# Few-key attention weights of two query blocks through one transpose, and the indexer's last pair in another PSUM pool

## The chip, the cores and the metric

The kernel runs on one core of one Trainium2 chip. The metric is the device time of one execution in microseconds (us), lower is better. A core has five instruction queues that run side by side, each strictly in its own order: TensorE (PE, matmuls, with its weight loads listed as PEld), VectorE (DVE), ScalarE (ACT), GpSimd (POOL) and SyncE (SP, which issues most transfers). Matmul results land in PSUM, which this kernel divides into eight buffers of 128 x 512 fp32: four "big" ones (pool `pm`, tile `mm`) and four "small" ones (pool `pa`, tile `at`).

## What is computed

One decoder layer on 256 tokens and 16 learned meta tokens in front of them (272 rows, width 2048). Cut to what the change touches:

```python
q, c_kv, q_idx, k_idx, w_idx, u = split_columns(h @ w_in)
score = einsum('bqhs,bqh->bqs', relu(q_idx . k_idx), w_idx)     # 16 indexer heads
_, sel = top_k(where(causal, score, -1e30), 64)
logits = q_abs . c_sel * HEAD_DIM**-0.5 + rel_bias[bucket(dist)]
p = softmax(logits);  o = p . c_sel;  attn = o @ w_uv           # 8 heads of 128
h = LN(alpha*h + concat(attn, pooled) @ w_o)                    # then a gated MLP and a second LN
```

The MLP (5632 wide, twice up and once down) is the larger part of the work; the change lies in the attention in front of it.

## The kernel before, in words

**Numbers.** Every fp32 product of the weights is made of three fast matmuls: operand a is split into a rounded upper part and the rest, and upper x upper, upper x rest and rest x upper are added in PSUM. Weights come from memory in blocks of 128 x 2048 (`wraw`); ACT writes the upper part (L127, two halves per block), DVE the rest (L128, two halves) into a ring of three `whl` buffers. `product` (L193) then issues 16 x 3 matmuls per block (L199, L200, L201). This runs through the whole kernel.

**Order.** The Tile layer places the instructions: it decides which buffer of a pool each tile gets, and in which order each queue holds its instructions. It is not written out by hand, so an edit of one tile can move others.

**Start.** PE runs 13 matmuls on a zeroed tile `warm` (L85 to L89) until the first input has been loaded and split. The first input blocks carry indexer key, head weights and the key/value latent (L264).

**Indexer.** Eight products, each for a pair of indexer heads, with the dots of the pair before in between (`dots`, L352: per head one matmul pair for each of the two query blocks, two ReLU copies on ACT, two accumulations on DVE into `score`). The eighth pair's dots come in the middle of the key projection (L403), in small buffers, like the projection itself (`kt`, L401).

**Two query blocks.** Queries 0 to 127 (block A) see 16 meta keys and 128 token keys (KA = 144); queries 128 to 255 (block B) see all 272 (KB). `score`, `bias` and the logits hold A's 144 columns and then B's 272 in one 416-wide row. The 64 largest scores per query are struck out in eight rounds on DVE (L444 to L448), L450 finds which are gone, and L452 adds -1e30 to the bias of the others, one instruction per head. The bias itself was laid out, mirrored, by three transfers (L345).

**Values.** `v0`, `v1`, `v2` (L413 to L439) are the values of the 16 meta keys, of the next 128 and of the last 128. `v0` holds the 16 rows three times, from partitions 0, 32 and 64 on (upper, rest, upper), in a zeroed tile of 80 rows; its counterpart for the weights, `ptx`, holds upper, upper, rest. One matmul with 80 rows gives all three products.

**Head loop (L585 to L611).** Eight heads, one per pass. In each pass PE runs one product for the pooling half of the layer (48 matmuls) and, between its slices, the attention steps of neighbouring heads: the logits of the next head (`softmax`, L489), `values` of the last head (L523) and `turn` of this head (L504). `softmax` scales and biases on DVE (L494), finds the largest logit per block (L497, A before B), ACT takes the exponential with its sum (L498), DVE divides (L501). `turn` transposes on PE: three 128 x 128 pieces (L506 to L508), and the 16 meta-key columns of A (L509) and of B (L510). ACT copies the big pieces (`pts`, L512) and the small ones twice into `ptx` (L518), DVE forms the rest (L520), POOL zeroes `ptx` first (L515). `values` (L526 to L528) multiplies them with `v0`, `v1`, `v2`. The pooling half follows in the same pass: ACT copies the finished product out (`u`, L549), POOL adds up windows (L553), DVE subtracts (L559), ACT and DVE split (L563, L564), and `pooled` (L566) multiplies every second pass. ACT then splits the next weight block (L127).

## Time and profile before

| | |
|---|---|
| median of 3 runs | 1045.23 us (1044.82 to 1045.94) |
| the profiled execution | 1045.81 us |
| its span, first to last instruction | 1044.0 us |
| mean granted TensorE clock | 0.997 |
| DVE, ACT, POOL busy | 85%, 60%, 19% of the span |

The profile is of one execution, so sums are made against its own 1045.81 us, 1.8 us of which lie outside the span; it is 0.6 us above the median. A matmul's row shows its whole latency; matmuls overlap, so what one costs is the distance from its start to the next start. In rows of a timeline the columns are start, length (of all that are merged), engine, line, operation, operands, shapes and count, then the idle time in front and what ended it. The head loop lies between about 140 and 211 us of the span, the indexer before 83 us, the MLP after about 304 us.

### The profile page before, as it was taken

The numbers are of one execution on the slowest core, as the hardware profiler recorded it, in microseconds if no ns is written. First come the engines' busy times: TensorE is split into PE (matmuls) and PEld (weight loads), VectorE is DVE, ScalarE is ACT, GpSimd is POOL, SyncE is SP. The second block draws the span as 40 slices with busy tenths as digits, with TensorE's granted clock in tenths as the row PEclk, the third lists the DMA queues.
The fourth block names the chain that finished last, engine by engine and source line by source line (L and its number), as shares of the span: only waits on it lengthen the run. The fifth ranks groups of instructions, "written<-read, shape, count | busy, mean of one in ns | idle before, by whom it ended". The sixth has DMA issues, their size and how long they took to land.

```text
span 1044.0 us, 19202 instructions
## 1 busy us (share of the span) xinstructions
PE 1034.6 (99%) x7639; PEld 984.2 (94%) x7639; DVE 888.2 (85%) x1401; ACT 623.2 (60%) x1000; POOL 194.8 (19%) x248
## 2 busy tenths in 40 slices
PE   9999999999999999999999999999999999999997
PEld 8999999999999999989999999999999999999986
DVE  6879568758779997799989989899898999999876
ACT  6666446645448855456565655656555666555665
POOL 1200014125340021211112111120111201220031
PEclk9999999999999999999999999999999999999998
DMA  8755643454554578789887787877878878787865
GB/s 319 256 180 216 226 145 117 146 189 164 180 196 149 175 223 238 235 291 298 278 285 274 262 291 267 287 273 269 281 268 287 275 277 278 268 286 270 292 214 159
DMA packets 59754, 250.28 MB, mean 240 GB/s; under 512 B 21734, under 2 KB 22416, under 8 KB 32656
## 3 DMA queue, kind: packets, MB, share of 16 engines
q1 hardware_dynamic: 34592, 230.42, 61.1%
q0 software_dynamic: 7888, 16.14, 8.2%
q10 hardware_dynamic: 17184, 2.49, 1.5%
q8 instruction: 60, 0.98, 0.4%
q14 instruction: 30, 0.25, 0.1%
HBM read 232.50 MB, written 2.11 MB: 225 GB/s over the span
## 4 chain that ended last, share of the span: by engine, by line
PE 85%; DVE 6%; issue 3%; DMA 3%; ACT 2%; POOL 1%; SPq 0%; POOLq 0%; DVEq 0%; ACTq 0%
PE mm L200 21%; PE mm L199 21%; PE mm L201 21%; PE at L785 5%; PE at L784 5%; PE at L786 5%; DVE whl L128 3%; DMA wraw<-in_w_first 1%; DMA wraw<-in_w_down 1%; ACT whl L127 1%; DMA wraw<-in_w_up 1%; DVE hp L705 0%; DVE x L700 0%; DVE x L701 0%; PE at L358 0%
## 5 line engine op out<-in xcount | busy, mean ns | idle before, releaser
L128 DVE TENSOR_TENSOR whl<-wraw,whl 128x1024 fp32r<-128x1024 f32 (+1 forms) x416 | 488.5, 1208 | 39.5 <-ACT whl L127 38.7
L127 ACT ACTIVATE whl<-wraw 128x1024 fp32r<-128x1024 f32 (+1 forms) x416 | 402.9, 1015 | 115.5 <-issue 27.1
L200 PE MATMUL mm<-hp,whl 128*128 128x258 f32 x1280 | 362.4, 283 | 0.7 <-DVE hp L705 0.7
L199 PE MATMUL mm<-hp,whl 128*128 128x258 f32 x1280 | 361.4, 282 | 0.0
L201 PE MATMUL mm<-hp,whl 128*128 128x258 f32 x1280 | 361.2, 282 | 0.0
L200 PEld LDWEIGHTS mm<-hp,whl 128*128 128x128 f32 x1280 | 242.7, 190 | 4.0 <-DVE hp L705 0.9
L199 PEld LDWEIGHTS mm<-hp,whl 128*128 128x128 f32 x1280 | 242.5, 189 | 3.2
L201 PEld LDWEIGHTS mm<-hp,whl 128*128 128x128 f32 x1280 | 242.9, 190 | 0.1
L199 PE MATMUL mm<-xp,whl 128*128 128x256 f32 (+5 forms) x384 | 111.9, 291 | 0.0
L200 PE MATMUL mm<-xp,whl 128*128 128x256 f32 (+5 forms) x384 | 108.7, 283 | 0.0
L201 PE MATMUL mm<-xp,whl 128*128 128x256 f32 (+5 forms) x384 | 108.7, 283 | 0.0
L719 ACT ACTIVATE z<-mm,cv 128x256 f32<-128x256 f32 x40 | 22.5, 563 | 95.6 <-PE mm L201 95.6
L199 PEld LDWEIGHTS mm<-xp,whl 128*128 128x128 f32 x384 | 72.4, 189 | 1.0 <-issue 0.5
L200 PEld LDWEIGHTS mm<-xp,whl 128*128 128x128 f32 x384 | 72.3, 188 | 0.4
L201 PEld LDWEIGHTS mm<-xp,whl 128*128 128x128 f32 x384 | 72.4, 188 | 0.3 <-DVE whl L128 0.2
L785 PE MATMUL at<-whl,gp 128*128 128x512 f32 x180 | 71.2, 396 | 0.8 <-DVE whl L128 0.8
L786 PE MATMUL at<-whl,gp 128*128 128x512 f32 x180 | 71.0, 395 | 0.0
L784 PE MATMUL at<-whl,gp 128*128 128x512 f32 x180 | 69.4, 395 | 0.0
L719 ACT ACTIVATE za<-mm,cv 128x256 f32<-128x256 f32 x40 | 22.5, 562 | 70.9 <-PE mm L201 66.2
L759 POOL TENSOR_TENSOR forms<-za 128x128 f32<-128x128 f32 x20 | 23.3, 1167 | 203.5 <-DVE za L737 203.5
L756 POOL TENSOR_TENSOR forms<-za 128x128 f32<-128x128 f32 x20 | 21.2, 1059 | 203.5 <-DVE za L737 139.1
L786 PEld LDWEIGHTS at<-whl,gp 128*128 128x128 f32 x180 | 33.8, 188 | 7.8
(346 smaller groups left out, 1925.4 us busy)
## 6 DMA issues: line engine op xcount, KB each, us to landing
wraw<-in_w_up SPq DMA_DIRECT2D x88, 1024.0 KB, 5.0
wraw<-in_w_down SPq DMA_DIRECT2D x80, 1024.0 KB, 6.8
wraw<-in_w_proj SPq DMA_DIRECT2D x24, 1024.0 KB, 5.0
wraw<-in_w_o SPq DMA_DIRECT2D x16, 1024.0 KB, 4.9
y<-v POOLq DMA_DIRECT2D x27, 256.0 KB, 8.5
y<-u POOLq DMA_DIRECT2D x18, 256.0 KB, 4.7
wraw<-in_w_first SPq DMA_DIRECT2D x8, 304.0 KB, 5.5
x<-in_xt SPq DMA_DIRECT2D x1, 2176.0 KB, 8.9
```

Source lines behind the costliest of these rows:

```text
L127: upper = nc.scalar.activation(hl[:, 0, c], raw[:, c], AF.Copy)
L128: lower = nc.vector.tensor_tensor(hl[:, 1, c], raw[:, c], hl[:, 0, c].bitcast(F32), op=ALU.subtract)
L199: nc.tensor.matmul(ps, wh, ah, start=n == 0, stop=False)
L200: nc.tensor.matmul(ps, wh, al, start=False, stop=False)
L201: nc.tensor.matmul(ps, wl, ah, start=False, stop=n == KT - 1)
L719: nc.scalar.activation(z, src[:, 2:NQ], AF.Identity, bias=col(C_B, j), scale=col(C_W, 3 * j + 2))
L756: nc.gpsimd.tensor_tensor(s[:, 0], a21, a22, op=ALU.add)
L759: nc.gpsimd.tensor_tensor(s[:, 3], a11, a21, op=ALU.subtract)
L784: nc.tensor.matmul(ps, a[:, 0, i], hl[:, 0, w], start=j == 0, stop=False)
L785: nc.tensor.matmul(ps, a[:, 0, i], hl[:, 1, w], start=False, stop=False)
L786: nc.tensor.matmul(ps, a[:, 1, i], hl[:, 0, w], start=False, stop=j == n - 1)
```

## The change

The diff does five things. Line numbers of the profile are those of the kernel before.

- **Warm-up:** the matmuls at the start read a constant that the program makes anyway, and there are 14 of them.
- **Last indexer pair:** its dots go to `big` buffers, not `small` ones.
- **Layout:** the 416-wide rows are B then A, so that B's 16 meta keys stand at the end of its 272 columns, right before A's 16 meta keys. For that `kt` gets the meta keys a second time at its end (a POOL copy), the bias has four transfers, and L450 becomes three instructions that put the pieces in the new order (`out_of`).
- **Turn:** one transpose of 32 columns replaces L509 and L510. Its 32 result rows are B's meta keys and A's; both blocks' columns need only one half of them. So `ptx` and `v0` have 96 rows, all written, in place of 80 with zeroed gaps; each copy is made per query block with a scale per partition (`of_block`, ones or zeros) that blanks the other block's rows: four ACT copies of 32 x 128 for two of 16 x 256, and two DVE instructions of 32 x 128 for one of 16 x 256. POOL's zeroing of `ptx` goes.
- **First two queries:** their weights (`lm`) get a row of 32 with zeros in its first half.

The order of PE's instructions is as before outside three places: the dots of the last pair, three matmuls of the first query product that now stand among the value matmuls, and the turn. On DVE the top-k rounds are no longer interrupted by two halves of a weight block (L128); one of them now stands right before the eight bias instructions and the other right behind. On ACT the exponential of the 272-wide block comes before that of the 144-wide one, and all four copies of a turn stand where the two stood.

```diff
@@ -82,10 +82,9 @@
         return pa.tile([P, 512], F32, tag="at", name="at")
 
 
-    warm = sb.tile([P, 256], mybir.dt.bfloat16, name="warm")
-    nc.gpsimd.memset(warm, 0.0)
+    warm = nc.const_aps.tensor(1.0, (P, 256), mybir.dt.bfloat16)
     ps = small()
-    for _ in range(13):
+    for _ in range(14):
         nc.tensor.matmul(ps[:, :256], warm[:, :P], warm, start=True, stop=True)
 
 
@@ -288,8 +287,9 @@
                                 compare_op=ALU.is_ge, fill=NEG, base=t0, channel_multiplier=1)
 
 
-    kt = ap_.tile([P, H, T], F32, name="kt")
-    ct = kt[:, H - 2:, :]
+
+    kt = ap_.tile([P, H, T + NM], F32, name="kt")
+    ct = kt[:, H - 2:, :T]
     sqs = []
     for j in range(2):
         ps = heads[1 + j][0]
@@ -342,18 +342,19 @@
         nc.vector.tensor_copy(strip[:, P:], ps[:H, :T])
         strip_d = dram.tile([H, STRIP], F32, name="strip_d")
         nc.gpsimd.dma_start(strip_d, strip)
-        for dst, n_rows, t0, n in ((bias[:, :, :KB], P, NM + P, KB), (bias[:, :, KB:], P, NM, KA), (bias_m, 2, Q0, NM)):
-
-            src = bass.AP(tensor=strip_d.tensor, offset=strip_d.offset + P + t0 - (n - 1),
+        for dst, n_rows, t0, s0, n in ((bias[:, :, :KA], P, NM, 0, KA), (bias[:, :, KA:KA + NM], P, NM + P, 0, NM),
+                                       (bias[:, :, KA + NM:], P, NM + P, NM, KB - NM), (bias_m, 2, Q0, 0, NM)):
+
+            src = bass.AP(tensor=strip_d.tensor, offset=strip_d.offset + P + t0 - s0 - (n - 1),
                           ap=[[1, n_rows], [STRIP, H], [1, n]])
             nc.gpsimd.dma_start(dst, src)
 
 
-    def dots(j, qi, pa_, heads):
+    def dots(j, qi, pa_, heads, buffer=small):
 
         for i in heads:
             h = 2 * j + i
-            pb = small()
+            pb = buffer()
             for o, n, t in ((pa_[:, S * i:S * i + S], S, slice(0, P)), (pb[:, :T], T, slice(P, S))):
                 nc.tensor.matmul(o, qi[:, i, t], kidx[:, 0, :n], start=True, stop=False)
                 nc.tensor.matmul(o, qi[:, i, t], kidx[:, 1 + i, :n], start=False, stop=True)
@@ -398,44 +399,46 @@
             nc.tensor.matmul(ps[:, :T], uk[:, 0, w], ctp[:, c, 0, :], start=c == 0, stop=False)
             nc.tensor.matmul(ps[:, :T], uk[:, 0, w], ctp[:, c, 1, :], start=False, stop=False)
             nc.tensor.matmul(ps[:, :T], uk[:, 1, w], ctp[:, c, 0, :], start=False, stop=c == 1)
-        nc.scalar.activation(kt[:, h, :], ps[:, :T], AF.Copy)
+        nc.scalar.activation(kt[:, h, :T], ps[:, :T], AF.Copy)
         if h == 2:
-            dots(7, qis[7], small(), (0, 1))
+            dots(7, qis[7], big(), (0, 1), big)
+    nc.gpsimd.tensor_copy(kt[:, :, T:], kt[:, :, :NM])
 
     y = sb.tile([P, KT, T], F32, tag="y", name="x", padded_shape=[P, KT, T])
     nc.sync.dma_start(y, xt)
     uv = weights()
 
-    few = ap_.tile([P, 2, 48], F32R, name="few")
-    nc.gpsimd.memset(few.bitcast(F32), 0.0)
-    for p in range(2):
-        nc.gpsimd.tensor_copy(few[:, :, 32 * p:32 * p + NM], ctp[:, :, p, :NM])
+    few = ap_.tile([P, 2, 4, NM], F32R, name="few")
+    for p in range(4):
+        nc.gpsimd.tensor_copy(few[:, :, p, :], ctp[:, :, p // 2, :NM])
     vs = []
     for i, (a, b) in enumerate(((0, NM), (NM, NM + P), (NM + P, T))):
         if i:
             v = ap_.tile([b - a, 1024], F32, name=f"v{i}", tag=f"v{i}")
         else:
 
-            v = ap_.tile([80, 1024], F32R, name="v0")
-            nc.gpsimd.memset(v.bitcast(F32), 0.0)
+            v = ap_.tile([96, 1024], F32R, name="v0")
         for g in range(2):
             ps = small()
             for c in range(2):
                 w = slice(1024 * c + 512 * g, 1024 * c + 512 * g + 512)
                 if i == 0:
-                    nc.tensor.matmul(ps[:48], few[:, c, :], uv[:, 0, w], start=c == 0, stop=False)
-                    nc.tensor.matmul(ps[:48], few[:, c, :], uv[:, 1, w], start=False, stop=c == 1)
+                    stack = few[:, c].rearrange("p a b -> p (a b)")
+                    nc.tensor.matmul(ps[:64], stack, uv[:, 0, w], start=c == 0, stop=False)
+                    nc.tensor.matmul(ps[:64], stack, uv[:, 1, w], start=False, stop=c == 1)
                     continue
                 nc.tensor.matmul(ps[:b - a], ctp[:, c, 0, a:b], uv[:, 0, w], start=c == 0, stop=False)
                 nc.tensor.matmul(ps[:b - a], ctp[:, c, 0, a:b], uv[:, 1, w], start=False, stop=False)
                 nc.tensor.matmul(ps[:b - a], ctp[:, c, 1, a:b], uv[:, 0, w], start=False, stop=c == 1)
             w = slice(512 * g, 512 * g + 512)
-            nc.scalar.activation(v[:b - a, w], ps[:b - a], AF.Copy)
-            if i == 0:
-                low = v[32:32 + NM, w]
-                nc.vector.tensor_tensor(low, ps[:NM], v[:NM, w].bitcast(F32), op=ALU.subtract)
-                nc.vector.tensor_tensor(low, ps[32:32 + NM], low.bitcast(F32), op=ALU.add)
-                nc.scalar.activation(v[64:64 + NM, w], ps[:NM], AF.Copy)
+            if i:
+                nc.scalar.activation(v[:, w], ps[:b - a], AF.Copy)
+            else:
+                low = v[32:64, w]
+                for r in (0, 64):
+                    nc.scalar.activation(v[r:r + 32, w], ps[:32], AF.Copy)
+                nc.vector.tensor_tensor(low, ps[:32], v[:32, w].bitcast(F32), op=ALU.subtract)
+                nc.vector.tensor_tensor(low, ps[32:64], low.bitcast(F32), op=ALU.add)
         vs.append(v)
 
 
@@ -447,9 +450,11 @@
             nc.vector.max(m8, src[:, a:b])
             nc.vector.match_replace(out=work[:, a:b], in_to_replace=m8, in_values=src[:, a:b], imm_value=REPLACED)
         src = work
-    nc.vector.tensor_tensor(work, work, score, op=ALU.is_equal)
+    out_of = temp([P, KW], "out_of")
+    for to, a, b in ((0, KA + NM, KW), (KB - NM, KA, KA + NM), (KB, 0, KA)):
+        nc.vector.tensor_tensor(out_of[:, to:to + b - a], work[:, a:b], score[:, a:b], op=ALU.is_equal)
     for h in range(H):
-        nc.vector.scalar_tensor_tensor(bias_of(h), work, NEG, bias_of(h), op0=ALU.mult, op1=ALU.add)
+        nc.vector.scalar_tensor_tensor(bias_of(h), out_of, NEG, bias_of(h), op0=ALU.mult, op1=ALU.add)
 
 
     qt = ap_.tile([P, H, NQ], F32, name="qt", tag="q")
@@ -464,7 +469,9 @@
     ps = small()
     for h in range(H):
         nc.tensor.matmul(ps[:2, h * NM:(h + 1) * NM], qt[:, h, :2], kt[:, h, :NM], start=True, stop=True)
-    lm = ap_.tile([2, H, NM], F32, name="lm")
+    both_few = temp([2, H * 2 * NM], "lm").rearrange("p (a b) -> p a b", b=2 * NM)
+    nc.gpsimd.memset(both_few, 0.0)
+    lm = both_few[:, :, NM:]
     nc.vector.scalar_tensor_tensor(lm, ps[:2, :H * NM].rearrange("p (a b) -> p a b", b=NM), scale,
                                    bias_m[:, :, ::-1], op0=ALU.mult, op1=ALU.add)
     mm = ap_.tile([2, 2, H], F32, name="mmeta")
@@ -474,50 +481,56 @@
     nc.vector.tensor_reduce(mm[:, 1, :], lm, axis=AX.X, op=ALU.add)
     nc.vector.reciprocal(mm[:, 1, :], mm[:, 1, :])
     nc.vector.tensor_tensor(lm, lm, mm[:, 1, :, None].to_broadcast([2, H, NM]), op=ALU.mult)
-    pm_sb = ap_.tile([NM, H, 2], F32, name="pm_sb")
+
+    pm_sb = ap_.tile([2 * NM, H, 2], F32, name="pm_sb")
+    of_block = ap_.tile([2 * NM, 2], F32, name="of_block")
+    for i in range(2):
+        nc.vector.tensor_reduce(of_block[:, i:i + 1], ident[:2 * NM, NM * i:NM * i + NM], axis=AX.X, op=ALU.add)
 
     def meta_weights():
         pmeta = small()
         for h in range(H):
-            nc.tensor.transpose(pmeta[:NM, 2 * h:2 * h + 2], lm[:, h, :], ident[:2, :2])
-        nc.vector.tensor_copy(pm_sb.rearrange("p a b -> p (a b)"), pmeta[:NM, :2 * H])
+            nc.tensor.transpose(pmeta[:2 * NM, 2 * h:2 * h + 2], both_few[:, h, :], ident[:2, :2])
+        nc.vector.tensor_copy(pm_sb.rearrange("p a b -> p (a b)"), pmeta[:2 * NM, :2 * H])
 
 
     mix = [None] * KT
-    AB = ((0, KA), (KA, KW))
+    BA = ((0, KB), (KB, KW))
 
     def softmax(h):
         ps = big()
-        nc.tensor.matmul(ps[:, :KA], qt[:, h, 2:2 + P], kt[:, h, :KA], start=True, stop=True)
-        nc.tensor.matmul(ps[:, KA:KW], qt[:, h, 2 + P:], kt[:, h, :], start=True, stop=True)
+        nc.tensor.matmul(ps[:, KB:KW], qt[:, h, 2:2 + P], kt[:, h, :KA], start=True, stop=True)
+        nc.tensor.matmul(ps[:, :KB], qt[:, h, 2 + P:], kt[:, h, NM:], start=True, stop=True)
         lg = temp([P, KW], "lg")
         nc.vector.scalar_tensor_tensor(lg, ps[:, :KW], scale, bias_of(h), op0=ALU.mult, op1=ALU.add)
         st = ap_.tile([P, 3, 2], F32, name="st", tag="st", bufs=2)
-        for i, (a, b) in enumerate(AB):
+        for i, (a, b) in enumerate(BA):
             nc.vector.tensor_reduce(st[:, 0, i:i + 1], lg[:, a:b], axis=AX.X, op=ALU.max, negate=True)
             nc.scalar.activation(lg[:, a:b], lg[:, a:b], AF.Exp, bias=st[:, 0, i:i + 1], accum_out=st[:, 1, i:i + 1])
         nc.vector.reciprocal(st[:, 2, :], st[:, 1, :])
-        for i, (a, b) in enumerate(AB):
+        for i, (a, b) in enumerate(BA):
             nc.vector.tensor_scalar_mul(lg[:, a:b], lg[:, a:b], st[:, 2, i:i + 1])
         return lg
 
     def turn(h, lg):
         pt, ptm = small(), small()
-        nc.tensor.transpose(pt[:, :P], lg[:, NM:KA], ident)
-        nc.tensor.transpose(pt[:, P:2 * P], lg[:, KA + NM:KA + NM + P], ident)
-        nc.tensor.transpose(pt[:, 2 * P:3 * P], lg[:, KA + NM + P:], ident)
-        nc.tensor.transpose(ptm[:NM, :P], lg[:, :NM], ident)
-        nc.tensor.transpose(ptm[:NM, P:2 * P], lg[:, KA:KA + NM], ident)
+        nc.tensor.transpose(pt[:, :P], lg[:, KB + NM:], ident)
+        nc.tensor.transpose(pt[:, P:2 * P], lg[:, :P], ident)
+        nc.tensor.transpose(pt[:, 2 * P:3 * P], lg[:, P:2 * P], ident)
+        nc.tensor.transpose(ptm[:2 * NM, :P], lg[:, 2 * P:2 * P + 2 * NM], ident)
         pts = temp([P, 3 * P], "pts")
         nc.scalar.activation(pts, pt[:, :3 * P], AF.Copy)
 
-        ptx = ap_.tile([80, NQ], F32R, name="ptx", tag="t", bufs=4, padded_shape=[P, KW])
-        nc.gpsimd.memset(ptx.bitcast(F32), 0.0)
+        ptx = ap_.tile([96, NQ], F32R, name="ptx", tag="t", bufs=4, padded_shape=[P, KW])
+        blocks = [(slice(2 + P * i, 2 + P * i + P), of_block[:, 1 - i:2 - i]) for i in range(2)]
         for r in (0, 32):
-            nc.vector.tensor_copy(ptx[r:r + NM, :2], pm_sb[:, h, :])
-            nc.scalar.activation(ptx[r:r + NM, 2:], ptm[:NM, :2 * P], AF.Copy)
-        nc.vector.tensor_tensor(ptx[64:64 + NM, :2], pm_sb[:, h, :], ptx[:NM, :2].bitcast(F32), op=ALU.subtract)
-        nc.vector.tensor_tensor(ptx[64:64 + NM, 2:], ptm[:NM, :2 * P], ptx[:NM, 2:].bitcast(F32), op=ALU.subtract)
+            nc.vector.tensor_copy(ptx[r:r + 32, :2], pm_sb[:, h, :])
+            for w, keep in blocks:
+                nc.scalar.activation(ptx[r:r + 32, w], ptm[:2 * NM, :P], AF.Copy, scale=keep)
+        nc.vector.tensor_tensor(ptx[64:, :2], pm_sb[:, h, :], ptx[:32, :2].bitcast(F32), op=ALU.subtract)
+        for w, keep in blocks:
+            nc.vector.scalar_tensor_tensor(ptx[64:, w], ptm[:2 * NM, :P], keep, ptx[:32, w].bitcast(F32),
+                                           op0=ALU.mult, op1=ALU.subtract)
         return pts, ptx
 
     def values(h, pts, ptx):
```

## Prediction

> **What bounds the kernel now.** First the page: its busy table and its chain of waits; then the stages of the head loop (start and end, then sum, and PE, PEld, DVE, ACT and POOL busy with their counts).
>
> ```profile
> PE 1034.6 (99%) x7639; PEld 984.2 (94%) x7639; DVE 888.2 (85%) x1401; ACT 623.2 (60%) x1000; POOL 194.8 (19%) x248
> ...
> PE 85%; DVE 6%; issue 3%; DMA 3%; ACT 2%; POOL 1%; SPq 0%; POOLq 0%; DVEq 0%; ACTq 0%
> ```
>
> ```profile
> 160.00:180.00 20.00, 20.00 (x159) 19.58 (x158) 17.65 (x38) 11.82 (x29) 10.31 (x11) 1.00 0.34 119
> 180.00:200.00 20.00, 20.00 (x162) 19.64 (x161) 15.27 (x42) 13.06 (x33) 3.31 (x7) 1.00 0.46 152
> ```
>
> PE is busy without a break, so an instruction less on PE is its slot less, and work added on DVE or ACT is free, as long as nothing that PE waits for comes late. By share ACT has 40% to spare here. But share is not slack: how late a result may come is read from the order of one pass. Here are ACT, then DVE, over one pass of the head loop (head 1 to head 2).
>
> ```profile
> 157.91 0.38 ACT L549 ACTIVATE u<-mm 128x272 f32<-128x272 f32 x1
> 158.19 1.99 ACT L127 ACTIVATE whl<-wraw 128x1024 fp32r<-128x1024 f32 x2
> ...
> 163.75 0.41 ACT L498 ACTIVATE lg<-lg,st 128x144 f32<-128x144 f32 x1 [1.62 <-DVE st L497]
> ...
> 164.67 0.47 ACT L512 ACTIVATE pts<-at 128x384 f32<-128x384 f32 x1
> 165.04 0.74 ACT L518 ACTIVATE ptx<-at 16x256 fp32r<-16x256 f32 x2
> 165.81 0.42 ACT L563 ACTIVATE df<-diff 128x258 fp32r<-128x258 f32 x1
> 166.14 0.37 ACT L549 ACTIVATE u<-mm 128x266 f32<-128x266 f32 x1
> ```
>
> ```profile
> 159.27 3.17 DVE L128 TENSOR_TENSOR whl<-wraw,whl 128x1024 fp32r<-128x1024 f32 x2 [0.70 <-ACT whl L127]
> 162.37 0.58 DVE L494 SCALAR_TENSOR_TENSOR lg<-mm,bias 128x416 f32<-128x416 f32 x1
> ...
> 163.42 0.64 DVE L497 TENSOR_REDUCE st<-lg 128x1 f32<-128x144 f32 x2
> ...
> 165.93 0.41 DVE L520 TENSOR_TENSOR ptx<-at,ptx 16x256 fp32r<-16x256 f32 x1
> ```
>
> These rows form a ring: u, then the weight split on ACT (L127), then on DVE (L128, which waited 0.70 us for it), the logits (L494), their maximum (L497), the exponential (L498, which waited 1.62 us for that), pts, ptx, df, and the next u. No step of it waited for PE. It took 166.14 - 157.91 = 8.23 us. PE's own pass is the distance of two `values`:
>
> ```profile
> 160.76 0.29 PE L526 MATMUL at<-ptx,v 80*128 80x258 f32 x1
> ...
> 168.72 0.28 PE L526 MATMUL at<-ptx,v 80*128 80x258 f32 x1
> ```
>
> That is 7.96 us. The ring is already slower than PE in this pass, with ptx done at 165.93 + 0.41 = 166.34 and PE asking for it at 168.72, 2.38 us later. Passes with the pooled product are longer for PE. Over six passes:
>
> ```profile
> 149.59 0.40 ACT L549 ACTIVATE u<-mm 128x272 f32<-128x272 f32 x1 [0.17 <-PE mm L201]
> ...
> 192.28 0.39 ACT L549 ACTIVATE u<-mm 128x262 f32<-128x262 f32 x1 [0.59 <-PE mm L201]
> ...
> 200.05 0.39 ACT L549 ACTIVATE u<-mm 128x260 f32<-128x260 f32 x1
> ```
>
> The ring needed 50.46 us from head 0 to head 6, and waited for PE 0.59 us of them, and by small gaps too short for a label about 0.2 us more. So it has 0.8 us in six passes, plus the reserve ahead of each `values`. At head 6:
>
> ```profile
> 200.06 0.41 DVE L520 TENSOR_TENSOR ptx<-at,ptx 16x256 fp32r<-16x256 f32 x1
> ```
>
> ```profile
> 202.30 0.28 PE L526 MATMUL at<-ptx,v 80*128 80x258 f32 x1
> ...
> 204.00 0.27 PE L508 MATMUL at<-ident,lg 128*128 128x128 f32 x1
> 204.11 0.27 PE L509 MATMUL at<-ident,lg 128*16 128x128 f32 x1
> 204.22 0.27 PE L510 MATMUL at<-ident,lg 128*16 128x128 f32 x1
> ```
>
> ptx is ready at 200.47, PE wants it at 202.30: 1.83 us.
>
> **The change part by part.** *PE.* A transpose holds PE for 0.11 us, from start to start in the last three rows, with 16 columns as with 128; so one with 32 costs the same. One less per head: 8 x 0.109 = **-0.87 us**.
>
> *ACT, the four copies.* The rows (operation, shapes, count, busy us and mean ns):
>
> ```profile
> L518 ACT ACTIVATE ptx<-at 16x256 fp32r<-16x256 f32 x16 | 5.9, 366 | 0.1
> L498 ACT ACTIVATE lg<-lg,st 128x272 f32<-128x272 f32 x8 | 4.1, 508 | 0.0
> ...
> L498 ACT ACTIVATE lg<-lg,st 128x144 f32<-128x144 f32 x8 | 3.3, 412 | 8.6 <-DVE st L497 8.6
> L530 ACT ACTIVATE mixa<-at 128x258 fp32r<-128x258 f32 x8 | 3.1, 387 | 8.4 <-PE at L528 8.4
> ...
> L576 ACT ACTIVATE mixp<-at,cv 128x258 fp32r<-128x258 f32 x6 | 2.7, 474 | 1.2 <-PE at L573 1.1
> ```
>
> 128 columns less are 508 - 412 = 96 ns less. L576 is L530 with a scale per partition: 87 ns more. A new copy is 366 - 96 + 87 = 357 ns, four are 1.43 us one by one; some will overlap by the 0.1 us by which pts and ptx do above (164.67 + 0.47 against 165.04). The old pair took 165.81 - 165.04 = 0.77. Added per head: 0.66 at most; none if all four overlapped and the scale were free (4 x 0.17 = 0.68). I take **+0.55**, nearer to the top, since the old pair didn't overlap. The Trainium skill, "ScalarE: Activation LUTs", section "What ACT_TABLE_LOAD costs", speaks against this edit: each per-partition operand adds about 93 ns to an ACTIVATE, and a fixed 186 ns stands beside 0.833 ns per element. The trace agrees with the first (87). By its fixed cost the old copy would be 399 ns; the trace has 366. By the page, as an estimate, four copies are 1.17 us with overlap against 0.61, which is +0.56.
>
> *DVE, the order of the blocks.* The first exponential now waits for the 272-wide maximum; rows of DVE:
>
> ```profile
> L497 DVE TENSOR_REDUCE st<-lg 128x1 f32<-128x272 f32 x8 | 3.4, 423 | 0.0
> ...
> L520 DVE TENSOR_TENSOR ptx<-at,ptx 16x256 fp32r<-16x256 f32 x8 | 3.3, 411 | 0.1
> ...
> L497 DVE TENSOR_REDUCE st<-lg 128x1 f32<-128x144 f32 x8 | 2.4, 294 | 0.0
> ```
>
> 423 - 294 = **+0.13** in the ring. The two halves of L520 cost about 0.35 each (0.41, less 0.13 for 128 columns as in L497, plus some for the scale): ptx is ready 0.29 later, outside the ring.
>
> *What the ring does then.* Each pass grows by 0.68 us (bounds 0.04 to 0.79), and the first u by 0.54, as head 0 has three copies between exponential and u in place of one (two more, 0.71, less the 0.17 that u waited). The u of head 6 comes at 149.59 + 0.54 + 50.46 - 0.8 + 6 x 0.68 = 203.87, its ptx 0.42 (as before) + 0.29 later, at 204.6. PE, seven transposes ahead, wants it at 202.30 - 0.76 = 201.54. It stands **3.0 us**. This is the sum over the loop, not per head: PE first touches the limit at head 2 (u at 149.59 + 0.54 + 16.55 + 2 x 0.68 = 168.04; ptx 0.20 + 0.29 later, at 168.53, against 168.72 - 0.33) and each later wait is part of the same shift. Behind a waiting `values` on PE stand the rest of the product and all that follows. Nothing gives it back: after the loop PE is the bound again.
>
> *Small buffers.* The eighth turn takes one of four, freed by DVE's last pass over the pooled result:
>
> ```profile
> 202.65 0.48 DVE L577 SCALAR_TENSOR_TENSOR mixp<-at,cv,mixp 128x258 fp32r<-128x258 f32 x1
> ```
>
> That end, 203.13, is u + 3.08, so 206.95; PE would be there at 204.11 - 0.76 + 3.0 = 206.35: **+0.6** (0 if the slot is another).
>
> *The rest.* The warm-up starts earlier, but the first real matmul waits for data, not for it. The dots of the last pair lose the wait shown next for a small buffer; they still wait for their query and for ACT's reading of the half that they share: -0.1 (0 to -0.3). The value matmuls of `v2` need a buffer that ACT frees, with two copies more ahead of it, 0.60 each as in the third row, which waited 0.80 for PE: 1.2 - 0.8 = 0.4 at most, and PE has three matmuls to fill in: +0.2 (0 to 0.4).
>
> ```profile
> 4.54 0.52 PE L268 MATMUL mm<-xp,whl 128*80 128x272 f32 x1 [0.48 <-ACT whl L223]
> ```
>
> ```profile
> 82.19 0.39 PE L358 MATMUL at<-kidx,qi 128*128 128x272 f32 x1 [0.15 <-ACT kt L401]
> ```
>
> ```profile
> 91.69 0.60 ACT L433 ACTIVATE v<-at 128x512 f32<-128x512 f32 x1 [0.80 <-PE at L431]
> ```
>
> The half of the weights done on DVE at 100.71 moves behind the eight bias instructions:
>
> ```profile
> 100.71 1.22 DVE L128 TENSOR_TENSOR whl<-wraw,whl 128x1024 fp32r<-128x1024 f32 x1
> ...
> 103.48 4.10 DVE L452 SCALAR_TENSOR_TENSOR bias<-work,bias 128x416 f32<-128x416 f32 x8
> ```
>
> ```profile
> 108.51 0.28 PE L201 MATMUL mm<-xp,whl 128*128 128x258 f32 x1
> ```
>
> The bias block ended at 107.58 with three such halves ahead of it; with one ahead it ends about 2.3 (2 x 1.22, overlapping a little) sooner, and about 0.2 later for L450 in three pieces. The moved half ends 1.22 after that, at 106.7, for PE's 108.51: hidden, with 1.8 us to spare. POOL's zeroing, transfers of the bias and the copy into `kt` lie tens of us ahead of their use.
>
> Sum: -0.87 + 3.0 + 0.6 - 0.1 + 0.2 = **+2.8 us**: the profiled execution from 1045.81 to 1048.6, the median from 1045.23 to **1048.0**.
>
> **The rivals.**
> - *The ring stays hidden, PE's gain is paid in full.* Below 0.23 us per pass (0.45 less, which is 3.0 over 6.7: six passes and the first u), no `values` waits. The point is ACT: four copies within about 0.9 us. For it: ACT is 60% busy; copies in a row can overlap. Against: the pair at 165.04 didn't. Time: 1045.23 - 0.87 = 1044.4, with the small terms 1044.2 to 1044.7.
> - *In between.* At 0.25 to 0.5 per pass PE waits 0.1 to 1.9 us: 1044.5 to 1046.8, middle 1045.6.
> - *More than the ring comes late.* Pooled results, small buffers and the late weight half each take a wait of their own, a us or two: 1050.
> - *The transpose isn't what it seems*: with 32 columns it costs PE as much as the two (a slot of 0.22), the ring as forecast: 1048.9.
>
> **How the numbers follow.** Forecast 0.48, hidden ring 0.18, in between 0.22, more late 0.08, no saving 0.04. With its bounds the forecast spans 1046.4 to 1049.2. The range leaves out the worst of the late case and little of the hidden one: 1044.2 to 1049.4. Within 0.2%, about what a measurement of this kernel tells from no change, is 1043.14 to 1047.32: the hidden ring, the middle, and a small part of the forecast (a ring of 0.50 to 0.57), together 0.46. Slower by over 0.2%: 0.50. Faster by over 0.2% would need twice the PE work that is removed: 0.04.
>
> **What would show it.** Right: waits of PE at `values` (the line that was L526) for DVE's ptx from head 2 to 4 on, some 3 us in all; u never waiting for PE after head 0; 32 ptx copies of about 350 ns with 0.25 to 0.37 from start to start; ring passes near 8.9. Wrong: four copies within 0.9 us, or ring passes as long as before; a stall at the value matmuls or at the third query product that outweighs the loop's; a transpose's slot other than 0.11.

## The result and the profile after

The changed kernel takes 1048.8 us (median of 7 runs, 1048.42 to 1050.07) against 1046.33 us for the kernel before in 7 runs: ratio 1.003, interval 1.002 to 1.004, so 2 to 4 us slower; the medians lie 2.47 us apart. In a second set of runs the same two gave 1.0035 (1.0023 to 1.0048). The profiled execution took 1048.8 us, 2.99 more than that of before; its span is 1046.9. Line numbers from here on are those of the kernel in question; in the changed one the names of the prediction are: weight split L126 (ACT) and L127 (DVE), logits L505, maximum L508, exponential L509, transposes L517 to L520, ptx L529 (ACT) and L532 (DVE), values L539 to L541, mixa L543 (ACT) and L544 (DVE), u L562, pooled L584 to L586, mixp L590.

First the page of the changed kernel: its busy table, and from its chain of waits the shares by engine.

```profile
PE 1034.6 (99%) x7632; PEld 983.7 (94%) x7632; DVE 889.8 (85%) x1413; ACT 626.6 (60%) x1016; POOL 195.0 (19%) x242
...
PE 80%; DVE 9%; DMA 3%; issue 3%; ACT 3%; POOL 2%; SPq 0%; POOLq 0%; DVEq 0%; ACTq 0%
```

PE has seven instructions less (eight transposes gone, one warm-up matmul more), yet the same busy time, and in the chain DVE has gone from 6% to 9%. The two stages of the head loop that the prediction showed, in the changed kernel (start and end, sum, then PE, PEld, DVE, ACT, POOL, the clock):

```profile
160.00:180.00 20.00, 18.16 (x130) 17.66 (x130) 16.69 (x37) 13.14 (x32) 8.25 (x9) 0.91 0.35 118
180.00:200.00 20.00, 20.00 (x161) 19.64 (x160) 15.99 (x38) 12.30 (x31) 3.87 (x5) 1.00 0.35 120
```

All of the loss is in the first: 130 matmuls where there were 159, PE idle for 1.84 us, and a clock of 0.91. What ACT did in one pass there (start, length of all merged, line):

```profile
157.10 1.22 ACT L529 ACTIVATE ptx<-at,of_block 32x128 fp32r<-32x128 f32 x4
...
158.67 0.38 ACT L562 ACTIVATE u<-mm 128x272 f32<-128x272 f32 x1
...
166.02 1.22 ACT L529 ACTIVATE ptx<-at,of_block 32x128 fp32r<-32x128 f32 x4
...
167.58 0.38 ACT L562 ACTIVATE u<-mm 128x266 f32<-128x266 f32 x1
```

The ring, u to u, is 8.91 us (8.92 in the table below, from unrounded times), where it was 8.23: the forecast was 8.9. But PE's rows show no wait at `values`. They show this one, in the pooled product of head 3:

```profile
171.22 0.28 PE L584 MATMUL at<-df,wpl 128*128 128x258 f32 x1
...
171.82 0.28 PE L586 MATMUL at<-df,wpl 128*128 128x258 f32 x1
173.94 0.39 PE L584 MATMUL at<-df,wpl 128*128 128x258 f32 x1 [1.84 <-DVE mixa L544]
```

173.94 - 171.82 is 2.12 us, a slot of 0.12 and 2.0 of waiting. The first of the two pooled results found a small PSUM buffer, the second did not; it takes the one that holds the value product, and that is free only when DVE has made `mixa` from it. DVE's rows of that time:

```profile
168.94 3.22 DVE L127 TENSOR_TENSOR whl<-wraw,whl 128x1024 fp32r<-128x1024 f32 x2 [0.61 <-ACT whl L126]
172.08 0.58 DVE L505 SCALAR_TENSOR_TENSOR lg<-mm,bias 128x416 f32<-128x416 f32 x1
172.58 0.41 DVE L572 SCALAR_TENSOR_TENSOR diff<-win,u 128x258 f32<-128x258 f32 x1
172.92 0.63 DVE L508 TENSOR_REDUCE st<-lg 128x1 f32<-128x272 f32 x2
173.47 0.41 DVE L544 TENSOR_TENSOR mixa<-at,mixa 128x258 fp32r<-128x258 f32 x1
```

`mixa` stands on DVE behind the whole row of ring steps (weight split, logits, maximum), although ACT's half of it, for which it waits, was done at 170.13:

```profile
169.76 0.37 ACT L543 ACTIVATE mixa<-at 128x258 fp32r<-128x258 f32 x1
```

When the ring is late, so is the buffer. In the kernel before, the same two instructions, DVE's and then PE's:

```profile
171.94 0.41 DVE L531 TENSOR_TENSOR mixa<-at,mixa 128x258 fp32r<-128x258 f32 x1
```

```profile
172.63 0.28 PE L571 MATMUL at<-df,wpl 128*128 128x258 f32 x1
```

L571 is the first matmul of the second pooled result, as L584 is in the changed kernel. The buffer was free at 172.35 and PE took it at 172.63: **0.28 us** in reserve, where `values` had 2.38 and 1.83. The wait adds up from this. From the third query product on the changed kernel runs 0.28 us ahead; counted from there, `mixa` ended 1.81 us later than before (173.88 + 0.28 - 172.35), and PE, four shorter turns ahead, was there 0.41 us sooner (172.63 - 171.94 - 0.28). From the end of `mixa` to PE's start it took 0.06. So 1.81 + 0.41 - 0.28 + 0.06 = 2.0. PE's own gain is more than the reserve that it had there.

Behind the wait came a second loss. The stages around it (the clock is the third figure from the end):

```profile
172.00:174.00 2.00, 0.16 (x2) 0.06 (x1) 1.97 (x8) 0.62 (x3) 0.00 (x0) 1.00 0.44 66
174.00:176.00 2.00, 2.00 (x12) 2.00 (x13) 1.11 (x6) 1.96 (x8) 0.00 (x0) 0.70 1.02 430
176.00:178.00 2.00, 2.00 (x11) 2.00 (x10) 1.97 (x6) 1.90 (x6) 0.00 (x0) 0.50 0.10 37
178.00:180.00 2.00, 2.00 (x16) 1.92 (x15) 1.30 (x3) 1.97 (x3) 1.69 (x3) 0.95 0.46 124
```

PE ran at half clock from 174.8 to 178.2 us: 11 matmuls in 2 us where there are 18 or 19.

Where the difference arose, by the starts of the same product in the two traces (changed less before): -0.76 us up to the eighth indexer product, -0.28 from the third query product on (dots and `v2` took 0.48), -0.56 at the product of head 3 (transposes gained), +2.53 at head 4, +2.81 at head 5, +2.67 from the end of the loop to 448 us, +3.15 behind a stall at 456 us, +2.9 at the end. I call what the difference grows by from the third query product to the product behind the loop the **loop cost**: here 2.67 + 0.28 = **+2.95 us**. It is free of what happens at the start and at 456 us, which differs between runs of one kernel; each kernel has one trace here, the changed one two.

### The profile page after: what moved, and what is told of

Same layout as the page of the kernel before. It is cut to its first block, busy times and chain, and to the rows that moved or that the text cites. A ratio compares the mean times of both kernels' runs of the same rounds, so it can differ in the third digit from the quotient of the medians.

```text
span 1046.9 us, 19201 instructions
## 1 busy us (share of the span) xinstructions
PE 1034.6 (99%) x7632; PEld 983.7 (94%) x7632; DVE 889.8 (85%) x1413; ACT 626.6 (60%) x1016; POOL 195.0 (19%) x242
## 4 chain that ended last, share of the span: by engine, by line
PE 80%; DVE 9%; DMA 3%; issue 3%; ACT 3%; POOL 2%; SPq 0%; POOLq 0%; DVEq 0%; ACTq 0%
PE mm L199 20%; PE mm L198 20%; PE mm L200 20%; PE at L798 5%; PE at L797 5%; PE at L799 5%; DVE whl L127 4%; DMA wraw<-in_w_down 2%; ACT whl L126 1%; POOL win L566 1%; DMA wraw<-in_w_up 1%; PE mm L269 1%; PE mm L268 0%; PE mm L267 0%; DVE hp L718 0%
## 5 line engine op out<-in xcount | busy, mean ns | idle before, releaser
L127 DVE TENSOR_TENSOR whl<-wraw,whl 128x1024 fp32r<-128x1024 f32 (+1 forms) x416 | 488.6, 1210 | 39.0 <-ACT whl L126 38.1
L126 ACT ACTIVATE whl<-wraw 128x1024 fp32r<-128x1024 f32 (+1 forms) x416 | 402.8, 1015 | 114.0 <-issue 27.1
L198 PEld LDWEIGHTS mm<-xp,whl 128*128 128x128 f32 x384 | 73.1, 190 | 1.0 <-issue 0.5
L199 PEld LDWEIGHTS mm<-xp,whl 128*128 128x128 f32 x384 | 73.1, 190 | 0.5
L200 PEld LDWEIGHTS mm<-xp,whl 128*128 128x128 f32 x384 | 73.1, 190 | 0.1
L772 POOL TENSOR_TENSOR forms<-za 128x128 f32<-128x128 f32 x20 | 26.2, 1311 | 205.5 <-DVE za L750 205.5
L769 POOL TENSOR_TENSOR forms<-za 128x128 f32<-128x128 f32 x20 | 21.2, 1059 | 201.0 <-DVE za L750 136.6
```

The costliest lines, as they stand in the source:

```text
L126: upper = nc.scalar.activation(hl[:, 0, c], raw[:, c], AF.Copy)
L127: lower = nc.vector.tensor_tensor(hl[:, 1, c], raw[:, c], hl[:, 0, c].bitcast(F32), op=ALU.subtract)
L198: nc.tensor.matmul(ps, wh, ah, start=n == 0, stop=False)
L199: nc.tensor.matmul(ps, wh, al, start=False, stop=False)
L200: nc.tensor.matmul(ps, wl, ah, start=False, stop=n == KT - 1)
L769: nc.gpsimd.tensor_tensor(s[:, 0], a21, a22, op=ALU.add)
```

## The experiments

Two theories to begin with. **Ring:** the ring is 0.69 us per pass longer, and whatever PE reads or takes behind it comes late; the pooled buffer is only the first place to show it. **Buffer:** the wait comes from the changed buffers and order, and would be there with a short ring. A third, **elsewhere:** the start, `v2` and the transfers make the difference. In the table, the waits are PE's, each less its normal slot.

| kernel | ring, head 1 to 2 | PE's waits in the loop | loop cost | ratio to before |
|---|---|---|---|---|
| before | 8.23 | none | 0 | 1 |
| changed | 8.92 | pooled 2.00, eighth turn 0.17; half clock | +2.95 | 1.003 |
| changed, again | 8.92 | pooled 1.99 and 0.56, turn 0.48 | +2.47 | 1.0035 |
| changed, A first | 8.78 | pooled 1.57 and 0.36, turn 0.26 | +1.54 | 1.0023 |
| changed, copy on GpSimd | 8.40 | none | -0.80 | 0.9997 |
| the same, and `v0` on GpSimd | 8.41 | none | -0.78 | 0.9993 |
| changed, pooled in large buffers | 8.92 | logits 1.46 and 0.59, values 0.43 | +1.95 | 1.0026 |
| changed, values in large buffers | 8.93 | values 1.05 and 1.55 | +1.93 | 1.003 |
| before, one copy twice | 8.77 | pooled 1.03 | +1.31 | 1.0022 |
| before, both copies twice | 8.91 | pooled 1.57 and 0.85, turn 0.68 | +3.52 | 1.0036 |
| before, both copies three times | 8.46 (then 12.2) | values 0.85, 2.47, 0.32, 4.20; half clock | +10.03 | 1.0109 |
| before, warm-up and dots changed | as before | none | +0.02 | 1.0001 |

**The ring alone, in the kernel before.**

```diff
-            nc.scalar.activation(ptx[r:r + NM, 2:], ptm[:NM, :2 * P], AF.Copy)
+            for _ in range(2):
+                nc.scalar.activation(ptx[r:r + NM, 2:], ptm[:NM, :2 * P], AF.Copy)
```

> The kernel before, in which ACT makes each of the two copies of the few weights twice (same data, same place): two ACT instructions of 0.37 us more per head, nothing else. Each ring pass grows by 0.74 us, 8.23 to about 8.97, as long as the changed kernel's 8.91, with no other part of the change there. Ring theory: PE waits 1.5 to 2.0 us at the second pooled product of head 3 (for DVE's mixa), a few tenths at later heads, and the span of before grows by 1.7 to 2.6, and by 1.6 more if the half clock comes: 1045.5 to 1048.2. Buffer theory (the wait belongs to the changed kernel's buffers and order of blocks): no wait there, 1043.0 to 1044.5.

Measured: 1048.46 us, ratio 1.0036 (1.0023 to 1.0048). The row of PE, and its waits over the loop (total, times, longest):

```profile
173.17 0.39 PE L572 MATMUL at<-df,wpl 128*128 128x258 f32 x1 [1.41 <-DVE mixa L532]
```

```profile
PE at L572 <- DVE mixa L532: 2.1, 2, 1.4
PE at L509 <- DVE mixp L578: 0.5, 1, 0.5
```

No layout, no buffer and no order of the change is in this kernel, only ACT work in the ring; the wait stands at the same instruction for the same releaser (L572 is L571 of the kernel before, since the edit adds a line). Its size comes out of the reserve: `mixa` is 1.80 us late here, and 1.80 - 0.28 + 0.05 is the 1.57 measured. The loop costs +3.52, above the expected 1.7 to 2.6: the waits at head 5 and at the eighth turn, 0.85 and 0.68, are more than the few tenths that I had for them. The buffer theory falls.

With one copy twice (`for _ in range(1 + r // 32)`):

> The kernel before with one of the two copies of the few weights made twice: +0.37 us per ring pass, 8.6. It fills the gap between the pass of before and the one of +0.74. From the waits of that kernel (1.57, 0.85 and 0.68 at heads 3, 5 and the eighth turn) the free time at these places is about 1.2, 1.8 and 1.9 us; a ring later by 1.3, 2.0 and 2.4 us there gives waits of 0.1 at head 3, 0.1 more at head 5, 0.3 more at the eighth turn: loop +0.2 to +0.6 on before. If the loop were ring-bound from the start (no free time), the cost is 6.7 x 0.37 = +2.5; if the cost were a fixed step of the changed buffers, 0.

Measured: 1047.28 us, ratio 1.0022 (1.0012 to 1.0031); loop +1.31, against 0.2 to 0.6 expected.

```profile
157.77 0.75 ACT L519 ACTIVATE ptx<-at 16x256 fp32r<-16x256 f32 x2
158.54 0.42 ACT L564 ACTIVATE df<-diff 128x258 fp32r<-128x258 f32 x1
158.99 0.37 ACT L519 ACTIVATE ptx<-at 16x256 fp32r<-16x256 f32 x1
159.39 0.40 ACT L550 ACTIVATE u<-mm 128x272 f32<-128x272 f32 x1
```

Two errors of mine: the extra copy was placed behind df, where nothing overlaps, so it cost 0.52 (first copy to u is 1.62 us; in the kernel before 166.14 - 165.04 = 1.10) and not 0.37; and I had taken 1.2 us of free time at head 3, worked out with too late a ring, where the rows above give 0.28. With 0.28 free, the ring 1.26 late there (`mixa` against before's, less this run's later start of 0.77) and 0.05 from the end of `mixa` to PE's start, the wait should be 1.03; it was 1.03. So even this one instruction per head is seen in the time.

With both copies three times (`range(3)`):

> The kernel before, in which ACT makes each of the two copies of the few weights three times: +1.48 us per ring pass, about 9.7. Ring theory: from the first heads on PE is bound by the ring; six passes of +1.48 and 1.3 at the first, less the 2.6 us of slack, give about +7.5 without any half clock, and more than 2.1 us of idle in one place (head 3 at the latest) brings at least one half clock window of 3.41 us, +1.6: span 1049 to 1054. Buffer theory: under 1046.

Measured: 1056.5 us, ratio 1.0109 (1.0095 to 1.0123), loop +10.03, more than the 9.1 expected. Here PE waits at `values`, as the prediction had it for the change (PE, then the stages):

```profile
205.66 0.28 PE L199 MATMUL mm<-xp,whl 128*128 128x260 f32 x1
209.98 0.36 PE L527 MATMUL at<-ptx,v 80*128 80x258 f32 x1 [4.03 <-DVE ptx L521]
```

```profile
207.00:210.00 3.00, 0.02 (x1) 0.05 (x1) 1.71 (x5) 2.93 (x7) 0.62 (x1) 1.00 0.00 0
210.00:212.00 2.00, 2.00 (x11) 1.94 (x12) 2.00 (x2) 0.95 (x2) 0.31 (x1) 0.74 0.00 0
212.00:214.00 2.00, 2.00 (x12) 1.85 (x11) 0.93 (x5) 1.24 (x4) 0.00 (x0) 0.50 0.42 66
```

**The ring shortened, in the changed kernel.** First by the order of the two blocks:

```diff
-    BA = ((0, KB), (KB, KW))
+    BA = ((KB, KW), (0, KB))
```

> The changed kernel with one line edited: the softmax takes the 144 columns of the first query block before the 272 of the second (as the kernel before did). Each ring pass (u to u) should get about 0.13 us shorter, 8.9 to 8.8. Ring theory (a longer ring delays DVE's mixa, which holds the small PSUM buffer that the second pooled product of head 3 needs; PE stands 2.0 us there and then runs 3.41 us at half clock): the wait shrinks by three to four passes' worth, 2.0 to 1.5 us, so the span of the changed kernel (1046.9) falls by 0.4 to 0.5, and by about 1.6 more if the shorter wait no longer brings the half clock: 1044.8 to 1046.5. Buffer theory (the wait comes from which buffer is asked for and not from the ring's length): wait and span as in the changed kernel, 1046.9.

Measured: 1047.53 us, ratio 1.0023 (1.0013 to 1.0032), profiled span 1045.4. The pass is 0.14 shorter, the wait 0.43, and the clock stays at 1.00:

```profile
172.00:174.00 2.00, 0.59 (x5) 0.52 (x5) 1.82 (x8) 1.22 (x5) 0.00 (x0) 1.00 0.56 143
174.00:176.00 2.00, 2.00 (x18) 2.00 (x18) 1.36 (x6) 1.96 (x7) 0.00 (x0) 1.00 0.93 389
```

Then by moving two of the four copies:

```diff
-        for r in (0, 32):
-            nc.vector.tensor_copy(ptx[r:r + 32, :2], pm_sb[:, h, :])
-            for w, keep in blocks:
-                nc.scalar.activation(ptx[r:r + 32, w], ptm[:2 * NM, :P], AF.Copy, scale=keep)
+        for w, keep in blocks:
+            nc.scalar.activation(ptx[:32, w], ptm[:2 * NM, :P], AF.Copy, scale=keep)
...
+        nc.gpsimd.tensor_copy(ptx[32:64, 2:], ptx[:32, 2:])
```

> The changed kernel with two of the four scaled copies of the few weights taken off ACT: GpSimd copies rows 32 to 63 of ptx from rows 0 to 31. ACT's ring should be shorter by about 0.6 us per pass, near the 8.2 of before. Ring theory: no wait at the second pooled product of head 3, no half clock, and PE's eight transposes are gained: span about 1046.9 - 2.0 - 1.6 = 1043.3, median about 1045.2, 0.8 to 1.2 below the kernel before. Buffer theory: the wait of 2.0 at the pooled product stays, and the half clock with it, 1046.9. Elsewhere theory (start, v2, transfers make most of the difference): 1046 or more whatever the ring does.

Measured: 1044.78 us against 1045.3 of before, ratio 0.9997 (0.9988 to 1.0006). The stage that lost everything:

```profile
172.00:174.00 2.00, 2.00 (x19) 2.00 (x18) 1.64 (x8) 1.69 (x7) 0.00 (x0) 1.00 0.84 283
174.00:176.00 2.00, 2.00 (x18) 2.00 (x18) 1.95 (x7) 2.00 (x7) 0.39 (x1) 1.00 0.57 238
```

PE waits for nothing in the loop, which costs -0.80 us: the eight transposes' gain. All else of the change is still in this kernel, the order of the blocks too. But it was close. DVE's rows, then PE's first matmul of the second pooled result:

```profile
168.20 2.79 DVE L127 TENSOR_TENSOR whl<-wraw,whl 128x1024 fp32r<-128x1024 f32 x2
...
172.41 0.42 DVE L545 TENSOR_TENSOR mixa<-at,mixa 128x258 fp32r<-128x258 f32 x1
```

```profile
172.95 0.31 PE L585 MATMUL at<-df,wpl 128*128 128x258 f32 x1
```

The buffer was free at 172.83, 0.12 us before PE took it, and DVE's weight split in front of it took 2.79 us, where it took 3.22 in the changed kernel and 3.13 in the one before. The shorter split came with this edit, and no run here says why. With a split as long as in the other two, as an estimate from these rows, 0.3 to 0.4 us of the 2.0 would have been left. So taking the two copies off ACT removes most of the wait, and the shorter split the rest; that copies on ACT alone bring such a wait is what the kernel before with its copies doubled shows. The span (1044.2) is 0.9 above the expected 1043.3, since this run started 1.03 us later than that of the changed kernel. That leaves the wait at `v2`:

```diff
-                for r in (0, 64):
-                    nc.scalar.activation(v[r:r + 32, w], ps[:32], AF.Copy)
+                nc.scalar.activation(v[:32, w], ps[:32], AF.Copy)
+                nc.gpsimd.tensor_copy(v[64:, w], v[:32, w])
```

> The changed kernel with both copies taken off ACT: rows 32 to 63 of ptx, and rows 64 to 95 of v0, copied by GpSimd. Ring theory: no wait in the loop (as in the version with ptx alone); the wait of 0.44 us at the value matmuls of v2 goes or falls to 0.1. From the first query product to the rest of the loop's products the gain over before is 0.8 + 0.1: 0.9 us; the median 0.3 to 1.0 below the kernel before on the same chip, within what the start differs between runs. If the v2 wait comes from something else than ACT's extra copy, 0.44 stays and the kernel is like the version with ptx alone.

In the changed kernel the value matmuls waited 0.44 us; a row of PE and one of ACT from it, then ACT's row with this edit:

```profile
90.98 0.51 PE L430 MATMUL at<-whl,ctp 128*128 128x512 f32 x1 [0.28 <-ACT v L435]
```

```profile
87.93 2.38 ACT L439 ACTIVATE v<-at 32x512 fp32r<-32x512 f32 x4
```

```profile
89.59 1.05 ACT L438 ACTIVATE v<-at 32x512 fp32r<-32x512 f32 x2
```

Measured: 1044.5 us against 1044.93, ratio 0.9993 (0.9984 to 1.0002). The wait at `v2` is gone; the part from the eighth indexer product to the third query product now gains 0.07 us instead of losing 0.48. This version is clearly faster than the changed kernel. In its trace the loop and `v2` are 0.85 us shorter than in the kernel before; the times do not show that it beats that kernel, since their interval holds 1, nor that it beats the version before it.

**Other buffers, ring as long as in the change.** Pooled results in the large pool (`ps = big()` at L581):

> The changed kernel with the pooled products' PSUM buffers from the large pool instead of the small one; the ring is as long as in the changed kernel (8.9). Ring theory: the wait at the second pooled product of head 3 goes, but the ring is still late and the next place shows it: values or the weight loads of a later head wait 1 to 3 us in all; span 1045.5 to 1047.5. Buffer theory: the wait goes and nothing takes its place: no half clock, 1043.3 to 1043.8.

Measured: 1048.2 us, ratio 1.0026 (1.0016 to 1.0036). PE's waits in the loop:

```profile
PE mm L502 <- DVE mixp L590: 1.7, 2, 1.3
PE at L539 <- DVE ptx L532: 0.3, 1, 0.3
```

The pooled result now holds a large buffer, and the logits stand behind DVE's `mixp`. Then the values in the large pool (`ps = big()` in `values`):

> The changed kernel with the PSUM of the value products taken from the large pool, so that no pooled product stands behind a mixa. The ring stays 8.9 per pass. Ring theory: the ring's delay is not the buffer's; with the pooled wait gone PE meets the ring where it reads ptx (values), as the prediction had it: waits there of 2.0 to 3.3 us in all over heads 2 to 6 (the kernel with the few weights copied three times waited 7.8 us at values for a ring that is 10.2 us late at head 6, so 2.4 are free; here it is 4.9 late at ptx and PE is 0.76 early). The loop costs +1.5 to +2.6 on before (start of the third query product to the rest's first) and the span is 1045.5 to 1047. Buffer theory: no wait of over 0.2 us in the loop, which costs -0.8, as in the version with the GpSimd copy: span 1043 to 1044.5.

Measured: 1047.95 us, ratio 1.003 (1.0019 to 1.0042).

```profile
186.66 0.36 PE L539 MATMUL mm<-ptx,v 96*128 96x258 f32 x1 [0.89 <-DVE ptx L532]
```

```profile
204.43 0.36 PE L539 MATMUL mm<-ptx,v 96*128 96x258 f32 x1 [1.39 <-DVE ptx L532]
```

Both waits are at `values`, 1.05 and 1.55 us by distance, 2.6 in all. Taking one buffer's wait away only sends PE on to the next result that is late. The loop costs 1.95 and 1.93 us in these two kernels, against 2.47 in the changed kernel without the half clock (next run): the ring makes PE wait, the buffers set the place, and they shift the sum by some 0.5 us.

**The half clock.** The changed kernel again:

> The changed kernel once more, on the chip of the other three. If the half clock is brought by the 2.0 us of idle, it comes again wherever the 3.41 us grid of the clock happens to lie, and the loop costs the same +2.95 (start of the third query product to start of the rest's first), span about 1046.9 less or more the 1 us by which the start differs between runs. If it hung on the phase of the grid, the same 2.0 us of wait comes with the clock at 1.0, and the loop costs about 1.6 less.

Measured: 1048.42 us, ratio 1.0035 (1.0023 to 1.0048). The same wait of 1.99 us, with the clock at 1.00:

```profile
175.58 0.39 PE L584 MATMUL at<-df,wpl 128*128 128x258 f32 x1 [1.83 <-DVE mixa L544]
```

```profile
174.00:176.00 2.00, 0.42 (x3) 0.42 (x4) 1.76 (x7) 0.98 (x5) 0.00 (x0) 1.00 0.53 111
176.00:178.00 2.00, 2.00 (x19) 2.00 (x18) 1.32 (x6) 1.96 (x8) 0.00 (x0) 1.00 0.99 410
```

So it does hang on the phase of the grid, the alternative in my text. But without it the loop costs only 0.5 less, not 1.6: PE comes earlier to the next late results and waits there (0.56 and 0.48, where the first trace has 0 and 0.17). While PE ran at half clock, the ring caught up. My ledger of 2.0 + 1.6 for the first trace added two things that are partly one.

**Warm-up and dots alone, in the kernel before** (constant tile, 14 matmuls; `dots(7, qis[7], big(), (0, 1), big)`).

> The kernel before with two parts of the change that do not touch the head loop: the warm-up from a constant tile (14 matmuls in place of 13) and the last pair's dots in the large PSUM buffers. From the two traces the start gave 0.76 us and the dots 0.2 to 0.3 at most: together 0.8 to 1.0 below the kernel before (span 1043.0 to 1043.2), if the start's gain is the warm-up's. If it is only the arrival of the first data, which differs from run to run, the span is 1043.8 to 1044.0. No wait at the pooled products of head 3 in either case.

Measured: 1045.31 us against 1045.3, ratio 1.0001 (0.9992 to 1.001). The dots gave 0.09. The start of this run was 0.21 earlier than that of before, but over all traces it lies between 1.03 earlier (a kernel with the old warm-up) and 0.89 later (one with the new): it is the run's, not the warm-up's. The 0.76 that the changed kernel's trace shows at its start was luck, and my expected 0.8 to 1.0 with it.

## Why the prediction was right and where it was wrong

- **The sum** came out close, +2.8 forecast, +2.99 between the profiled executions, and 3.1 (2 to 4) by the ratio, but not by the path that I described, and in part by luck. The +2.99 holds an early start (-0.76) and a longer stall at 456 us (+0.48), which differ between runs, and the half clock, which the sum did not have. Between the fixed points of the loop the forecast was 3.0 + 0.6 - 0.87 = +2.7; measured are +2.95 with the half clock and +2.47 without.
- **The ring** was right in path and size: 8.91 forecast, 8.91 measured, and the kernels before with copies doubled, which change nothing else, show that it is the cause. Its terms: the copies cost 1.24 us against 0.77 (first copy to df), +0.47 where I took +0.55; the mean copy is 349 ns (I took 357). Two copies to the same rows start 0.25 us apart and so overlap by 0.09; from rows 0 to 31 to rows 32 to 63 they start 0.36 apart and don't overlap, like the old pair (0.37). The order of the blocks cost 0.14 where I took 0.13. Some 0.08 per pass stand in DVE's weight split, 3.26 us (from 160.03) against 3.17 (from 159.27); no run shows why. By the Trainium skill's "ScalarE: Activation LUTs", section "What ACT_TABLE_LOAD costs", the estimate was +0.56; the trace stays below it.
- **The step that failed** is "What the ring does then": "PE first touches the limit at head 2" and "It stands 3.0 us", at `values`, counted from a reserve of 1.83 to 2.38 us there. I read the reserve at one consumer only. A shorter one, 0.28 us, lay at the second pooled product, whose buffer is freed by an instruction queued behind the ring on DVE; under "Small buffers" I looked at the eighth turn only and put nothing for this one. So the wait came at head 3, at `pooled`, 2.0 us, and there was none at `values`. Where that place is taken away, PE does wait at `values`, 2.6 us where I had 3.0. The working let the ring grow by 0.23 us per pass before PE waits; at `pooled`, by the rows above and as an estimate, a ring as long as before already means 0.41 - 0.28 + 0.06 = 0.2 us of wait. The rival "More than the ring comes late" named the pooled results, but as waits on top of the one at `values`.
- **The eighth turn** (+0.6 forecast): 0.17 in the first trace, 0.48 in the second. The mechanism is as described, the size is what other waits leave of it.
- **v2** (+0.2 forecast, 0 to 0.4): 0.44, just above the bound; the extra copies are the cause, shown by removing them. **Dots** (-0.1): -0.09.
- **Transposes** (-0.87): -0.80, seen where nothing waits. The rival that a 32-column transpose saves nothing falls: its slot is 0.11.
- **Warm-up** (0): right, though the trace of the changed kernel alone seemed to speak against it.
- **Moved weight half** (hidden): no stall of DVE or PE showed there. POOL's zeroing of `ptx` did not lie tens of us ahead of its use, as I wrote, but about 2 (162.98, with ACT's copy at 165.04); nothing hung on it.
- **Not foreseen:** the half clock, worth 0.5 us between the two traces of the changed kernel.

## What to carry to other kernels

When work is added to an engine that is "60% busy", find the closed chain of steps it stands in, and then read the reserve at *every* place where PE takes something that the chain delivers: results that it reads, and PSUM buffers that an instruction queued behind the chain must free. The smallest reserve decides where the wait appears. Giving that place another buffer moved the wait here and took off 0.5 us of some 2.5; it did not remove it. Removing 0.8 us of PE work showed in the loop only once the added copies were on an engine outside the chain.

## What the runs showed of the hardware

**The clock falls on a grid, and less than a whole stretch of idle is enough.** In the trace of the changed kernel the clock's record turns to full at 4.12 us, and the half-speed stretch runs from 174.79 to 178.20, 3.413 us long and 50 such stretches after 4.12. I counted PE's idle time within each stretch of that grid, in the head loop and near 458 us, each wait less its normal slot:

| trace | idle within one stretch of 3.41 us | the next stretch |
|---|---|---|
| changed (wait all in one) | 2.00 | half clock |
| before, copies three times (second stretch of the 4.20 wait) | 2.44 | half clock |
| the same (first stretch of that wait) | 1.75 | full |
| changed, at 458 us | 1.69 | full |
| changed again (wait cut in two by the grid) | 1.57 | full |
| A first | 1.57 | full |

In these rows the switch lies between 1.75 and 2.00 us of idle in one stretch. The same wait of 2.0 us costs the clock or not by where the grid falls.

The ends of the traces show a limit of that count. In all twelve the clock falls once more near the end, 301 to 305 whole stretches after its record first turns to full. The stretch in front of that fall has between 0.97 us (`v0` on GpSimd too) and 2.28 us without any row of PE. The smallest of these hold two matmuls with one row (`1*128 1x512`); without those all twelve have 2.02 to 2.54 us. Whether such matmuls count as idle for the clock, no run here tests, so 1.75 to 2.00 is shown only for stretches without them.

The Trainium skill, "TensorE: Matmul & The Clock Gate", section "What's actually happening", has these stretches as windows of 3413 ns, free-running, and the traces agree (3.413 us); its section "Why this matters for your kernels" asks for no idle gap over about 3 us, and here the measurement decides: 2.0 us was enough.

**Starts differ.** The record of the clock turns to full between 4.1 and 9.8 us in these traces, and the eighth indexer product's start varies by 1.9 us between runs, whichever the warm-up. It turns up on the same grid: in all twelve traces the stretch in front holds at most 0.48 us without a row of PE (before, 3.13 to 6.54). Behind stretches with 0.64 us (copy on GpSimd, 1.89 to 5.31) and 0.88 us (`v0` on GpSimd too, 2.97 to 6.39) PE stayed slow for one more, with matmuls of 0.43 us that take 0.29 later. A difference of a few tenths in the total can't be read from one execution of each kernel; compared between two fixed points inside it, 0.1 us can.
